# A convolution module in which ScalarE and VectorE follow the written order and SyncE issues every copy

## Chip, cores and metric

The kernel runs on one core of a Trainium2 chip. The metric is device time in microseconds (us) of one execution; the profile's span is the stretch from the first to the last instruction of one profiled execution.

## What is computed

A two-layer decoder trunk on 256 tokens of width 1024, in float32. Each layer has a half-step SwiGLU feed-forward network (FFN, inner width 2816), a token mixer, and a second FFN. The mixer of layer 0 is the Conformer convolution module, which the change is about; that of layer 1 is stick-breaking attention. The module computes, with h the normalized input:

```python
val, gate = split(h @ w_pw1 + b_pw1, 2)
u = val * sigmoid(gate)
u = depthwise_causal_conv(u, w_dw, width=31) + b_dw
u = silu(layer_norm(u, ln_g, ln_b))
x = x + u @ w_pw2 + b_pw2
```

## The kernel before

Tokens lie in T = 2 tiles of 128. All large products are made in pieces: each float32 weight is loaded as `raw` and split into a rounded part `hi` (a cast on ScalarE, line 144) and the rest `lo` (a subtraction on VectorE, line 145), and `mm3` (lines 180 to 182) adds three matmuls, hi x hi, lo x hi, hi x lo, into one PSUM tile. `raw` has three buffers, `hi` and `lo` six each, for the whole kernel. SyncE (SP in the profile) issues the loads of the weights.

The module (`conv`) has 1024 channels, in eight blocks k of 128 (up, acc, sk). Its steps are:

- **U(e, t)**, for four chunks e of w_pw1 and two token tiles t: 24 matmuls with the chunk's two halves (four k each), then ScalarE copies the sum to `vg`, scaled (line 401). Each U leaves a **gate** behind: four transposes of vg on PE (line 406), and for the chunk's two channel blocks a sigmoid `sg` on ScalarE (line 409) and a multiply-add `up` on VectorE (line 410). The gate of one U is put into the middle of the next U (after nine matmuls) or of the next taps.
- **shifted(k, ...)**: four copies, SBUF to SBUF, by DMA of `up[k]` to `sk[k]`, which lays four shifted copies of 32 channels over the partitions (line 441). Odd k are issued by ScalarE, even k by SP.
- **weights(e)**: two VectorE products `wb` (line 426), the banded weights of the convolution.
- **taps(k, tb, nt)**: the depthwise convolution of a block as matmuls of sk[k] with wb (line 451), 64 rows in the trace, then `acc` is copied from PSUM by ScalarE with the bias (line 457). The first four blocks are done for both token tiles at once, the last four once for each tile. The narrow ones take turns on two PSUM buffers with U.
- **norm_in, norm, turn, out_mm**: transposes of acc and `bn_stats` (line 470), the layer norm as two VectorE steps `z` and a sigmoid times z (`m`, lines 484 to 489), transposes of m and a split to `xT` (line 496), the second product (lines 180 to 182) and its addition to x (line 509).
- **boundary**: the normalized, transposed input of the next FFN.

The program order at the end of `conv` decides what is issued when: inside `tc.manual_schedule` the engines named in its list take their instructions as written. Before, that list is PE and SP. ScalarE, VectorE and GpSimd are ordered by the framework's scheduler when the kernel is built. Each engine then runs its own list strictly in order. A tile whose buffer is not yet free makes the instruction that writes it wait.

Of the kernel before, what the change touches and what calls it, by code (L numbers as in the profile page):

```python
# [8 lines left out]
F32 = mybir.dt.float32  # L9
F32R = mybir.dt.float32r  # L10
# [4 lines left out]
P = 128  # L15
D = 1024
KD = D // P
T = 2
DFF = 2816
# [13 lines left out]
def trunk_kernel(  # L33
# [7 lines left out]
    nc = tc.nc  # L41
# [97 lines left out]
    def nm(s):  # L139
        uid[0] += 1  # L140
        return f"{s}_{uid[0]}"

    def split(hi, lo, src, eng=None, copy=nc.scalar.copy):
        copy(hi, src)  # L144
        (eng or nc.vector).tensor_tensor(lo, src, hi.bitcast(F32), op=ALU.subtract)  # L145
# [20 lines left out]
    def load_pairs(w, c0, c1, n, **kw):  # L166

        wv = w.rearrange("(k p) n -> p k n", p=P)
        return [
            load_w([wv[:, 4 * h : 4 * h + 4, c : c + n] for c in (c0, c1)], [4, 2, n], **kw) for h in range(2)  # L170
        ]

    def load_rows(w, k0, **kw):

        wv = w.rearrange("(k p) n -> p k n", p=P)
        hi, lo = load_w([wv[:, k0 : k0 + 2, :]], [2, 1, D], **kw)
        return hi[:, :, 0, :], lo[:, :, 0, :]
# [33 lines left out]
    def u_mm(t, hT, units, n, between=None):  # L211
        ps = ps_u.tile([P, 512], F32, tag="u", name=nm("psu"))
        h, l, _ = hT
        for k in range(KD):
            wh, wl = units[k // 4]
            mm3(ps[:, :n], h[:, k, :], l[:, k, :], wh[:, k % 4], wl[:, k % 4], k == 0, k == KD - 1)
            if between is not None and k == 2:
                between()
        return ps
# [153 lines left out]
        return outs  # L373


    def conv(hTs, next_gi):
        H = TAPS
        SW = H - 3 + T * P
        acc = [
# [2 lines left out]
        up, sks, wbs, vunits = [], {}, [], []  # L382
        units = {}

        def load_chunk(e):
            units[e] = load_pairs(conv_w_pw1[0], 2 * e * P, D + 2 * e * P, 2 * P, pieces=4)

        def load_out(c):
            vunits.append(load_rows(conv_w_pw2[0], 2 * c))

        pending = []

# [2 lines left out]
            if pending:  # L395
                pending.pop()()

        def U(e, t):
            ps = u_mm(t, hTs[t], units[e], 512, between=finish)
            vg = wk.tile([P, 4, P], F32, tag="B", bufs=4, name=nm("vg"))  # L400
            nc.scalar.activation(vg, ps, AF.Copy, scale=hTs[t][2])

            def gate():
                pt = ps_t.tile([P, 4, P], F32, tag="tr", name=nm("ptr"))
                for q in range(4):
                    nc.tensor.transpose(pt[:, q, :], vg[:, q, :], ident)
                for q, k in enumerate((2 * e, 2 * e + 1)):
                    s = wk.tile([P, P], F32, tag="sg", name=nm("sg"))
                    nc.scalar.activation(s, pt[:, 2 + q, :], AF.Sigmoid, bias=vec[:, B1 + 8 + k : B1 + 9 + k])
                    nc.vector.scalar_tensor_tensor(  # L410
                        up[k][:, H + t * P : H + (t + 1) * P],
                        pt[:, q, :], vec[:, B1 + k : B1 + k + 1], s, op0=ALU.add, op1=ALU.mult,
                    )
                    if e == 3:
                        shifted(k, *((0, SW - P), (SW - P, SW))[t])
                    elif t == T - 1:
                        shifted(k, 0, SW)

            pending.append(gate)

        def weights(e):

            wb = ring.tile([P, 2, 32, 32], F32, tag=("hi", "lo")[e % 2], name=nm("wb"))
            for i in range(2):
                k = 2 * e + i
                nc.vector.tensor_tensor(
                    wb[:, i],
                    ind.unsqueeze(1).broadcast_to([P, 32, 32]),
                    wq[:, 4 * k : 4 * k + 4, :].rearrange("p g m -> p (g m)").unsqueeze(2)
                    .broadcast_to([P, 32, 32]),  # L430
                    op=ALU.mult,
                )
            wbs.append(wb)

        def shifted(k, a, b):

            if k not in sks:
                sks[k] = wk.tile([P, 4, SW], F32, tag="sk", bufs=4, name=nm("sk"))
            for g in range(4):
                v = up[k][32 * g : 32 * g + 32, a:b]  # L440
                (nc.scalar if k % 2 else nc.sync).dma_start(
                    sks[k][:, g, a:b], bass.AP(tensor=v.tensor, offset=v.offset, ap=[v.ap[0], [1, 4], [1, b - a]])
                )

        def taps(k, tb, nt, pool, tag):
            wb, sk = wbs[k // 2][:, k % 2], sks[k]
            pc = pool.tile([P, nt * P], F32, tag=tag, name=nm("pc"))
            for m in range(8):
                for g in range(4):
                    c = 4 * m + tb * P  # L450
                    nc.tensor.matmul(  # L451
                        pc[32 * g : 32 * g + 32, :], wb[:, 8 * g + m, :], sk[:, g, c : c + nt * P],
                        start=m == 0, stop=m == 7,
                    )
                if m == 3:
                    finish()
            nc.scalar.activation(
                acc[k][:, tb * P : (tb + nt) * P], pc, AF.Identity, bias=vec[:, BD + k : BD + k + 1]
            )
# [3 lines left out]
        def norm_in(t, q):  # L463

            if t not in stats:
                stats[t] = wk.tile([P, 2, 6], F32, tag="st", name=nm("st"))
            pl = ps_v.tile([P, 4, P], F32, tag=f"v{t}{q}", name=nm("pl"))
            for i in range(4):
                nc.tensor.transpose(pl[:, i, :], acc[4 * q + i][:, t * P : (t + 1) * P], ident)
            nc.vector.bn_stats(stats[t][:, q, :], pl.rearrange("p k c -> p (k c)"))  # L470
            pls[t, q] = pl
# [28 lines left out]
        def out_mm(t, n):  # L500
            ns = slice(n * 512, (n + 1) * 512)
            pv = ps_v.tile([P, 512], F32, tag=f"v{t}{n}", name=nm("psv"))
            for k in range(KD):
                wh, wl = vunits[k // 2]
                mm3(
                    pv, xT[:, t, k, 0, :], xT[:, t, k, 1, :], wh[:, k % 2, ns], wl[:, k % 2, ns],
                    k == 0, k == KD - 1,
                )
            nc.vector.tensor_tensor(xt[t][:, ns], pv, xt[t][:, ns], op=ALU.add)

        for _ in range(KD):
            up.append(wk.tile([P, H + T * P], F32, tag="A", bufs=13, name=nm("up")))
            nc.gpsimd.memset(up[-1][:, :H], 0.0)
        outs = []


        with tc.manual_schedule(engines={mybir.EngineType.PE, mybir.EngineType.SP}):
            load_chunk(0)
            load_chunk(1)
            U(0, 0)  # L520
            weights(0)
            U(0, 1)
            load_chunk(2)
            U(1, 0)
            weights(1)
            load_chunk(3)
            U(1, 1)
            b2 = wk.tile([P, D], F32, tag="sc4", name="b2")
            nc.sync.dma_start(b2, conv_b_pw2[0:1, :].broadcast_to([P, D]))
            taps(0, 0, T, ps_v, "v01")  # L530
            U(2, 0)
            load_out(0)
            taps(1, 0, T, ps_v, "v11")
            weights(2)
            U(2, 1)
            for t in range(T):
                nc.vector.tensor_tensor(xt[t], xt[t], b2, op=ALU.add)
            taps(2, 0, T, ps_v, "v01")
            U(3, 0)
            weights(3)  # L540
            for c in range(1, 4):
                load_out(c)
            taps(3, 0, T, ps_v, "v11")
            U(3, 1)
            taps(4, 0, 1, ps_v, "v01")
            norm_in(0, 0)
            taps(5, 0, 1, ps_v, "v11")
            taps(6, 0, 1, ps_u, "u")
            taps(7, 0, 1, ps_u, "u")
            taps(4, 1, 1, ps_u, "u")  # L550
            norm_in(0, 1)
            norm(0)
            taps(5, 1, 1, ps_u, "u")
            norm_in(1, 0)
            taps(6, 1, 1, ps_u, "u")
            turn(0, 0)
            taps(7, 1, 1, ps_u, "u")
            turn(0, 1)
            norm_in(1, 1)
            norm(1)  # L560
            out_mm(0, 0)
            out_mm(0, 1)
            for q in range(2):
                turn(1, q)
            out_mm(1, 0)
            outs.append(boundary(0, next_gi))
            out_mm(1, 1)
        outs.append(boundary(1, next_gi))
        return outs


    def attention(hTs, next_gi):
# [155 lines left out]
    ]  # L728
    hTs.append(boundary(1, 0))
    hTs = ffn(0, 0, 0, hTs, 1, first=first, hook=load_conv_consts)  # L730
    hTs = conv(hTs, 2)
    hTs = ffn(0, 1, 2, hTs, 3)
    hTs = ffn(1, 0, 3, hTs, 4)
    hTs = attention(hTs, 5)
    nc.sync.dma_start(fg, final_g.rearrange("(o d) -> o d", o=1).broadcast_to([P, D]))
# [27 lines left out]
```

## Time and profile before

| | |
|---|---|
| Time, median of 3 runs | 1014.5 us (1012.63 to 1016.3) |
| Profiled execution, own time | 1018.19 us |
| Its span | 1016.3 us |
| PE busy | 984.6 us |
| VectorE (DVE) busy | 710.4 us |
| ScalarE (ACT) busy | 515.3 us |
| mean granted clock of TensorE | 0.992 |
| convolution module on PE | about 202 us to 329 us of the span |

Reading it: a row of the timeline has the start in us, the duration, the engine, the line, the operation and `out<-in`, then how often it is repeated; in brackets stands how long the engine was idle before it and which instruction ended the wait. ACTq and SPq are the sequencers of ScalarE and SP issuing DMAs; while ScalarE issues, it does nothing else. Matmuls overlap, so the start-to-start distance is what one costs.

### The profile page before, as it was taken

How to read it: one execution, taken by the hardware profiler on the slowest of the kernel's cores; microseconds unless marked ns; L12 is line 12 of the kernel's file. 1: busy time of each engine (PE TensorE's matmuls, PEld its weight loads, DVE VectorE, ACT ScalarE, POOL GpSimd, SP SyncE). 2: the span in 40 equal slices, each digit the busy share in tenths (PEclk: the TensorE clock that was granted, in tenths of full speed). 3: DMA queues.
4: the chain of work that ended last, by engine and by line, in shares of the span. 5: the costliest groups of instructions: out<-in, count | busy, mean ns of one | idle time of the engine just before them, and what ended most of it. 6: DMA issues, size and time to landing. Idle time of an engine off the chain costs nothing.

```text
span 1016.3 us, 14823 instructions
## 1 busy us (share of the span) xinstructions
PE 984.6 (97%) x5710; PEld 816.8 (80%) x5710; DVE 710.4 (70%) x1094; ACT 515.3 (51%) x870; POOL 142.6 (14%) x173
## 2 busy tenths in 40 slices
PE   6999999998889999999999999999999999999997
PEld 5888888875578888888888888888777678888885
DVE  6977777845346877776787777777767986767664
ACT  5654545433333645454555454555644554545432
POOL 5011111100000111111111111111210011111111
PEclk9999999998989999999999999999999999999999
DMA  8857564434652764747465647474625346555511
GB/s 272 295 181 251 171 230 148 158 97 141 193 192 68 244 227 148 234 145 238 148 188 165 227 148 235 145 235 145 190 87 180 108 129 203 180 193 190 183 42 42
DMA packets 143111, 177.76 MB, mean 175 GB/s; under 512 B 6392, under 2 KB 126272, under 8 KB 143040
## 3 DMA queue, kind: packets, MB, share of 16 engines
q1 hardware_dynamic: 139808, 173.93, 52.8%
q10 hardware_dynamic: 3232, 2.88, 1.1%
q8 instruction: 45, 0.74, 0.3%
q14 instruction: 26, 0.21, 0.1%
HBM read 171.08 MB, written 1.05 MB: 169 GB/s over the span
## 4 chain that ended last, share of the span: by engine, by line
PE 87%; DMA 4%; DVE 3%; ACT 2%; issue 1%; SPq 1%; ACTq 1%; POOL 0%; POOLq 0%; DVEq 0%
PE psc L228 28%; PE psc L229 16%; PE psv L180 8%; PE psv L182 8%; PE psv L181 8%; PE psc L231 4%; PE psu L180 3%; PE psu L181 2%; PE psu L182 2%; PE pc L451 2%; DMA raw<-in_conv_w_pw_dram 2%; DMA raw<-in_ffn_w_in_dram 2%; DVE lo L145 1%; ACT hi L144 1%; PE pz L620 1%
## 5 line engine op out<-in xcount | busy, mean ns | idle before, releaser
L145 DVE TENSOR_TENSOR lo<-raw,hi 128x1024 fp32r<-128x1024 f32 (+1 forms) x352 | 398.2, 1150 | 117.5 <-ACT hi L144 117.0
L228 PE MATMUL psc<-xT,hi 128*128 128x512 f32 x1232 | 443.0, 398 | 0.6 <-DVE u L234 0.6
L144 ACT CAST hi<-raw 128x1024 fp32r<-128x1024 f32 (+1 forms) x356 | 327.6, 960 | 106.8 <-PE psc L228 35.2
L229 PE MATMUL psc<-xT,lo 128*128 128x256 f32 x1408 | 366.7, 281 | 0.0
L229 PEld LDWEIGHTS psc<-xT,lo 128*128 128x128 f32 x1408 | 265.6, 189 | 16.0 <-issue 0.4
L228 PEld LDWEIGHTS psc<-xT,hi 128*128 128x128 f32 x1232 | 231.8, 188 | 50.8 <-DVE u L234 1.0
L289 POOL TENSOR_TENSOR s<-s,rrow 128x256 f32<-128x256 f32 x80 | 93.9, 1173 | 585.1 <-DVE s L288 585.1
L180 PE MATMUL psv<-hi,ah 128*128 128x512 f32 x352 | 137.6, 391 | 0.1
L181 PE MATMUL psv<-lo,ah 128*128 128x512 f32 x352 | 137.2, 390 | 0.0
L182 PE MATMUL psv<-hi,al 128*128 128x512 f32 x352 | 136.9, 390 | 0.0
L233 ACT COPY u<-psc 128x256 f32<-128x256 f32 x176 | 65.2, 371 | 132.1 <-PE psc L231 131.7
L234 DVE TENSOR_TENSOR u<-psc,u 128x256 f32<-128x256 f32 x176 | 74.0, 421 | 79.3 <-ACT u L233 78.7
L144 ACT CAST ah<-s 128x256 fp32r<-128x256 f32 x80 | 32.6, 407 | 95.8 <-DVE s L291 95.8
L181 PEld LDWEIGHTS psv<-lo,ah 128*128 128x128 f32 x352 | 66.1, 188 | 14.0
L182 PEld LDWEIGHTS psv<-hi,al 128*128 128x128 f32 x352 | 66.1, 188 | 13.9
L180 PEld LDWEIGHTS psv<-hi,ah 128*128 128x128 f32 x352 | 66.1, 188 | 12.9 <-ACT ah L144 1.0
L231 PE MATMUL psc<-xT,hi 128*128 128x512 f32 x176 | 70.0, 398 | 0.0
L180 PE MATMUL psu<-hi,xT 128*128 128x512 f32 x160 | 65.0, 406 | 0.0
L181 PE MATMUL psu<-lo,xT 128*128 128x512 f32 x160 | 63.3, 396 | 0.0
L182 PE MATMUL psu<-hi,xT 128*128 128x512 f32 x160 | 63.0, 394 | 0.0
L287 ACT ACTIVATE s<-u 128x256 f32<-128x256 f32 x80 | 33.3, 416 | 46.5 <-DVE u L285 46.5
L145 DVE TENSOR_TENSOR al<-s,ah 128x256 fp32r<-128x256 f32 x80 | 33.5, 419 | 21.8 <-ACT ah L144 21.8
(128 smaller groups left out, 791.2 us busy)
## 6 DMA issues: line engine op xcount, KB each, us to landing
raw<-in_ffn_w_in_dram SPq DMA_DIRECT2D x172, 512.0 KB, 4.7
raw<-in_ffn_w_out_dram SPq DMA_DIRECT2D x44, 1024.0 KB, 4.9
raw<-in_conv_w_pw_dram SPq DMA_DIRECT2D x16, 512.0 KB, 4.5
raw<-in_attn_w_qkv_dram SPq DMA_DIRECT2D x16, 512.0 KB, 4.6
raw<-in_conv_w_pw_dram SPq DMA_DIRECT2D x4, 1024.0 KB, 7.9
raw<-in_attn_w_qkv_dram SPq DMA_DIRECT2D x4, 1024.0 KB, 5.1
raw<-in_attn_w_o_dram SPq DMA_DIRECT2D x4, 1024.0 KB, 4.9
raw<-in_ffn_w_in_dram SPq DMA_DIRECT2D x8, 256.0 KB, 5.8
```

What stands on the lines that cost most here:

```text
L144: copy(hi, src)
L145: (eng or nc.vector).tensor_tensor(lo, src, hi.bitcast(F32), op=ALU.subtract)
L180: nc.tensor.matmul(ps, lh, rh, start=start, stop=False)
L181: nc.tensor.matmul(ps, lh, rl, start=False, stop=False)
L182: nc.tensor.matmul(ps, ll, rh, start=False, stop=stop)
L228: nc.tensor.matmul(ps, h, xT[:, :, k, :, :], start=k == 0, stop=False)
L229: nc.tensor.matmul(ps[:, :, 0, :], l, xT[:, :, k, 0, :], start=False, stop=False)
L231: nc.tensor.matmul(ps, h, xT[:, :, k, :, :], start=False, stop=True)
L233: nc.scalar.copy(u, ps[:, :, 1, :])
L234: nc.vector.tensor_tensor(u, ps[:, :, 0, :], u, op=ALU.add)
L287: nc.scalar.activation(a, u, AF.Sigmoid)
L289: nc.gpsimd.tensor_tensor(a, a, rrow, op=ALU.mult)
```

## The change

All of it is in `conv` and its two callers:

- the list of engines in `manual_schedule` now names ScalarE and VectorE too;
- loading and casting a weight unit are two functions, `fetch_*` and `cast`, called at different places: the fetch of a half chunk stands some steps ahead, its cast inside the U of the chunk before it, behind that U's gate and any `weights` (through the new arguments of U);
- all copies of `shifted` are issued by SP;
- the fetches and casts of the next FFN's first unit (both halves) stand inside `conv`, and the FFN is handed the result;
- the addition of b_pw2 to x stands behind taps(5, 0).

```diff
-    def conv(hTs, next_gi):
+    def conv(hTs, next_gi, next_w):
...
+        def fetch(srcs, shape):
+            raw = rawp.tile([P, *shape], F32, tag="raw", name=nm("raw"))
+            for c, src in enumerate(srcs):
+                nc.sync.dma_start(raw[:, :, c, :], src)
+            return [raw, shape]
+
+        def cast(unit):
+            raw, shape = unit
+            hi = ring.tile([P, *shape], F32R, tag="hi", name=nm("hi"))
+            lo = ring.tile([P, *shape], F32R, tag="lo", name=nm("lo"))
+            for k in range(shape[0]):
+                split(hi[:, k], lo[:, k], raw[:, k])
+            unit[:] = hi, lo
...
-        def U(e, t):
-            ps = u_mm(t, hTs[t], units[e], 512, between=finish)
+        def U(e, t, *todo):
+            def between():
+                finish()
+                for f, *args in todo:
+                    f(*args)
+
+            ps = u_mm(t, hTs[t], units[e], 512, between=between)
...
-                (nc.scalar if k % 2 else nc.sync).dma_start(
+                nc.sync.dma_start(
...
-        with tc.manual_schedule(engines={mybir.EngineType.PE, mybir.EngineType.SP}):
-            load_chunk(0)
-            load_chunk(1)
-            U(0, 0)
-            weights(0)
-            U(0, 1)
-            load_chunk(2)
-            U(1, 0)
-            weights(1)
-            load_chunk(3)
-            U(1, 1)
...
+        E = mybir.EngineType
+        with tc.manual_schedule(engines={E.PE, E.SP, E.Activation, E.DVE}):
+            fetch_in(0, 0)
+            fetch_in(0, 1)
+            fetch_in(1, 0)
+            for unit in units[0]:
+                cast(unit)
+            fetch_in(1, 1)
+            fetch_in(2, 0)
+            U(0, 0, (cast, units[1][0]))
+            fetch_in(2, 1)
+            U(0, 1, (cast, units[1][1]))
+            fetch_in(3, 0)
+            U(1, 0, (weights, 0), (cast, units[2][0]))
+            fetch_in(3, 1)
             b2 = wk.tile([P, D], F32, tag="sc4", name="b2")
             nc.sync.dma_start(b2, conv_b_pw2[0:1, :].broadcast_to([P, D]))
+            U(1, 1, (cast, units[2][1]))
+            fetch_out(0)
             taps(0, 0, T, ps_v, "v01")
-            U(2, 0)
-            load_out(0)
+            U(2, 0, (weights, 1), (cast, units[3][0]))
+            fetch_out(1)
             taps(1, 0, T, ps_v, "v11")
-            weights(2)
-            U(2, 1)
+            U(2, 1, (cast, units[3][1]))
+            fetch_out(2)
+            taps(2, 0, T, ps_v, "v01")
+            U(3, 0, (weights, 2), (cast, vunits[0]), (cast, vunits[1]))
+            fetch_out(3)
+            nxt.append(fetch_chunk(next_w, 0, DFF, 0))
+            taps(3, 0, T, ps_v, "v11")
+            U(3, 1, (weights, 3), (cast, vunits[2]))
+            nxt.append(fetch_chunk(next_w, 0, DFF, 1))
+            taps(4, 0, 1, ps_v, "v01")
+            norm_in(0, 0)
+            cast(vunits[3])
+            taps(5, 0, 1, ps_v, "v11")
             for t in range(T):
                 nc.vector.tensor_tensor(xt[t], xt[t], b2, op=ALU.add)
...
             taps(7, 0, 1, ps_u, "u")
+            cast(nxt[0])
             taps(4, 1, 1, ps_u, "u")
...
             out_mm(0, 0)
+            cast(nxt[1])
             out_mm(0, 1)
...
-    hTs = ffn(0, 1, 2, hTs, 3)
+    hTs, first = conv(hTs, 2, ffn_w_in[0, 1])
+    hTs = ffn(0, 1, 2, hTs, 3, first=first)
```

How the order moves, at three places. The numbers behind the names tell buffers apart and are not the same in both programs.

ScalarE around the U of chunk 1 and token tile 1 and the first taps, before (vg_2127 and vg_2194 are the copies of U(1,0) and U(1,1), hi_2133 and hi_2146 the two halves of chunk 3, acc_1909 the result of the first taps):

```order
L441 DMA sk_2107<-up_1919 128x1x284 x4
L401 ACTIVATE vg_2127<-psu_2081,rstd_285_1862 128x512
L409 ACTIVATE sg_2173<-ptr_2168,vec 128x128
L409 ACTIVATE sg_2176<-ptr_2168,vec 128x128
L144 CAST hi_2133<-raw_2132 128x512 x4
L401 ACTIVATE vg_2194<-psu_2158,rstd_293_1907 128x512
L144 CAST hi_2146<-raw_2145 128x512 x4
L409 ACTIVATE sg_2220<-ptr_2215,vec 128x128
L457 ACTIVATE acc_1909<-pc_2198,vec 128x256
```

and now (vg_2120 and vg_2173 are the copies of U(1,0) and U(1,1), hi_2095 and hi_2148 the halves of chunk 2, hi_2245 the first half of chunk 3):

```order
L144 CAST hi_2095<-raw_1967 128x512 x4
L425 ACTIVATE vg_2120<-psu_2061,rstd_285_1862 128x512
L433 ACTIVATE sg_2142<-ptr_2137,vec 128x128
L433 ACTIVATE sg_2145<-ptr_2137,vec 128x128
L144 CAST hi_2148<-raw_2007 128x512 x4
L425 ACTIVATE vg_2173<-psu_2127,rstd_293_1907 128x512
L433 ACTIVATE sg_2199<-ptr_2194,vec 128x128
L433 ACTIVATE sg_2207<-ptr_2194,vec 128x128
L481 ACTIVATE acc_1909<-pc_2177,vec 128x256
L144 CAST hi_2245<-raw_2058 128x512 x4
```

The four copies are gone from ScalarE's list, and the cast ahead of the vg of U(1,1) is now that of chunk 2; the cast of chunk 3 stands behind the first taps.

ScalarE around the layer norm of token tile 0, before (acc_1913 to acc_1916 are blocks 4 to 7, here from the narrow taps; m_2765 and m_2771 the sigmoids of norm(0); hi_3110 the second half of the next FFN's first unit; xT the split of turn):

```order
L457 ACTIVATE acc_1916<-pc_2684,vec 128x128
L457 ACTIVATE acc_1913<-pc_2718,vec 128x128
L457 ACTIVATE acc_1914<-pc_2776,vec 128x128
L488 ACTIVATE m_2765<-z_2764 128x512
L144 CAST hi_3110<-raw_3109 128x512 x3
L488 ACTIVATE m_2771<-z_2770 128x512
L457 ACTIVATE acc_1915<-pc_2817,vec 128x128
L144 CAST hi_3110<-raw_3109 128x512
L144 CAST xT<-ptr_2851 128x4x128
L457 ACTIVATE acc_1916<-pc_2858,vec 128x128
```

and now (hi_2724 is the first half of the next FFN's first unit):

```order
L481 ACTIVATE acc_1916<-pc_2690,vec 128x128
L144 CAST hi_2724<-raw_2457 128x512 x4
L481 ACTIVATE acc_1913<-pc_2734,vec 128x128
L512 ACTIVATE m_2781<-z_2780 128x512
L512 ACTIVATE m_2787<-z_2786 128x512
L481 ACTIVATE acc_1914<-pc_2792,vec 128x128
L481 ACTIVATE acc_1915<-pc_2833,vec 128x128
L144 CAST xT<-ptr_2867 128x4x128
L481 ACTIVATE acc_1916<-pc_2874,vec 128x128
```

acc_1914, the result of taps(5,1), stood ahead of both sigmoids and now stands behind both; four casts now stand between the last acc of tile 0 and the first of tile 1.

SP around the copies of the last pair of blocks, before (sk_2499 is block 6; raw_2450 to raw_2466 are pieces of w_pw2, raw_3096 and raw_3109 the next FFN's first unit):

```order
L159 DMA raw_2450<-in_conv_w_pw_dram 128x2x1024
L159 DMA raw_2458<-in_conv_w_pw_dram 128x2x1024
L159 DMA raw_2466<-in_conv_w_pw_dram 128x2x1024
L441 DMA sk_2499<-up_1929 128x1x156 x4
L159 DMA raw_3096<-in_ffn_w_in_dram 128x4x256 x2
L159 DMA raw_3109<-in_ffn_w_in_dram 128x4x256 x2
L159 DMA raw_3122<-in_ffn_w_out_dram 128x2x1024
L441 DMA sk_2499<-up_1929 128x1x128 x4
```

and now (sk_2485 and sk_2493 are blocks 6 and 7, raw_2455 the last piece of w_pw2, raw_2457 and raw_2551 the next FFN's first unit):

```order
L388 DMA raw_2455<-in_conv_w_pw_dram 128x2x1024
L388 DMA raw_2457<-in_ffn_w_in_dram 128x4x256 x2
L465 DMA sk_2485<-up_1929 128x1x156 x4
L465 DMA sk_2493<-up_1931 128x1x156 x4
L388 DMA raw_2551<-in_ffn_w_in_dram 128x4x256 x2
L465 DMA sk_2485<-up_1929 128x1x128 x4
L465 DMA sk_2493<-up_1931 128x1x128 x4
```

Both blocks' copies now stand in this one list, sixteen with two loads between them, and the first FFN loads stand ahead of them.

## Rows read from the trace of the kernel before

**Rows 1.** The page, its first part: busy time, share, instructions.

```profile
PE 984.6 (97%) x5710; PEld 816.8 (80%) x5710; DVE 710.4 (70%) x1094; ACT 515.3 (51%) x870; POOL 142.6 (14%) x173
```

**Rows 2.** Waits with PE waiting, 196 to 345 us: total, times, longest.

```profile
PE ptr L406 <- ACT vg L401: 10.2, 3, 5.0
PE pc L451 <- ACT acc L457: 3.0, 1, 3.0
```

**Rows 3.** Timeline of PE: first and second pause.

```profile
223.31 0.66 PE L406 MATMUL ptr<-ident,vg 128*128 128x128 f32 x4 [0.91 <-ACT vg L401]
...
233.52 1.12 PE L406 MATMUL ptr<-ident,vg 128*128 128x128 f32 x4 [4.24 <-ACT vg L401]
...
239.22 0.39 PE L180 MATMUL psu<-hi,xT 128*128 128x512 f32 x1
```

**Rows 4.** Timeline of PE: the same place at full clock, to the next taps.

```profile
255.96 0.66 PE L406 MATMUL ptr<-ident,vg 128*128 128x128 f32 x4
...
259.23 0.40 PE L180 MATMUL psu<-hi,xT 128*128 128x512 f32 x1
...
264.12 1.93 PE L451 MATMUL pc<-sk,wb 128*32 128x256 f32 x32
```

**Rows 5.** Timeline of PE: third and fourth pause, and full clock between.

```profile
280.27 1.11 PE L406 MATMUL ptr<-ident,vg 128*128 128x128 f32 x4 [5.05 <-ACT vg L401]
...
283.18 0.66 PE L469 MATMUL pl<-ident,acc 128*128 128x128 f32 x4
283.76 5.45 PE L451 MATMUL pc<-sk,wb 128*32 128x128 f32 x192
292.16 2.55 PE L451 MATMUL pc<-sk,wb 128*32 128x128 f32 x64 [2.95 <-ACT acc L457]
...
298.08 0.66 PE L469 MATMUL pl<-ident,acc 128*128 128x128 f32 x4
```

**Rows 6.** Busy time by stretch; the first number after POOL is the granted clock.

```profile
234.00:236.00 2.00, 2.00 (x19) 0.98 (x22) 1.98 (x4) 1.82 (x4) 0.00 (x0) 0.50 0.01 2
254.00:256.00 2.00, 2.00 (x34) 0.98 (x33) 0.72 (x1) 0.69 (x1) 0.00 (x0) 1.00 0.00 0
294.00:296.00 2.00, 2.00 (x28) 1.27 (x23) 0.21 (x1) 0.37 (x1) 0.56 (x3) 0.50 0.98 333
```

**Rows 7.** Timeline of ScalarE: copies issued, a cast, acc, a sigmoid of the norm.

```profile
218.58 3.95 ACTq L441 DMA_DIRECT2D sk<-up  x4
...
230.71 2.18 ACT L144 CAST hi<-raw 128x512 fp32r<-128x512 f32 x4 [5.49 <-DMA raw<-in_conv_w_pw_dram]
...
287.61 3.83 ACTq L441 DMA_DIRECT2D sk<-up  x4
291.49 0.88 ACT L457 ACTIVATE acc<-pc,vec 128x128 f32<-128x128 f32 x3 [4.62 <-issue]
...
300.59 0.63 ACT L488 ACTIVATE m<-z 128x512 f32<-128x512 f32 x1
```

**Rows 8.** SP's timeline; the tile sk; issues by line with KB and landing.

```profile
257.54 4.29 SPq L441 DMA_DIRECT2D sk<-up  x4
...
L441 SPq DMA_DIRECT2D sk<-up x20: 542/602/2024, 217.8 to 289.3; - x20
...
DMA to landing us min/median/max: 2.2/4.0/6.5
...
raw<-in_conv_w_pw_dram SPq DMA_DIRECT2D x4, 1024.0 KB, 7.9
```

**Rows 9.** Timeline of VectorE: lo behind the cast of rows 7; norm(0).

```profile
231.36 2.50 DVE L145 TENSOR_TENSOR lo<-raw,hi 128x512 fp32r<-128x512 f32 x4 [5.75 <-ACT hi L144]
...
295.79 0.70 DVE L470 BATCH_NORM_STATS2 st<-pl 128x6 f32<-128x512 f32 x1 [7.62 <-PE pl L469]
...
299.14 0.69 DVE L489 TENSOR_TENSOR m<-z,m 128x512 f32<-128x512 f32 x1
299.75 0.75 DVE L487 SCALAR_TENSOR_TENSOR z<-z,lnr,lnb 128x512 f32<-128x512 f32 x1
```

More of the change, by code (lines that the diff above doesn't have):

```diff
@@ L383, in conv, with fetch_chunk, fetch_in, fetch_out @@
         units = {}
[L385 to L389, printed above, removed]
+        def fetch(srcs, shape):
[10 more added lines that the diff above has]
+            unit[:] = hi, lo
+        def fetch_chunk(w, c0, c1, h):
+            wv = w.rearrange("(k p) n -> p k n", p=P)
+            return fetch([wv[:, 4 * h : 4 * h + 4, c : c + 2 * P] for c in (c0, c1)], [4, 2, 2 * P])
+        def fetch_in(e, h):
+            units.setdefault(e, []).append(fetch_chunk(conv_w_pw1[0], 2 * e * P, D + 2 * e * P, h))
+        def fetch_out(c):
+            wv = conv_w_pw2[0].rearrange("(k p) n -> p k n", p=P)
+            vunits.append(fetch([wv[:, 2 * c : 2 * c + 2, :]], [2, 1, D]))
         pending = []
@@ L505, in out_mm @@
                 mm3(
-                    pv, xT[:, t, k, 0, :], xT[:, t, k, 1, :], wh[:, k % 2, ns], wl[:, k % 2, ns],
+                    pv, xT[:, t, k, 0, :], xT[:, t, k, 1, :], wh[:, k % 2, 0, ns], wl[:, k % 2, 0, ns],
                     k == 0, k == KD - 1,
@@ L513, in conv @@
             nc.gpsimd.memset(up[-1][:, :H], 0.0)
-        outs = []
-        with tc.manual_schedule(engines={mybir.EngineType.PE, mybir.EngineType.SP}):
-            load_chunk(0)
-            load_chunk(1)
-            U(0, 0)
-            weights(0)
-            U(0, 1)
-            load_chunk(2)
-            U(1, 0)
-            weights(1)
-            load_chunk(3)
-            U(1, 1)
+        outs, nxt = [], []
+        E = mybir.EngineType
[13 more added lines that the diff above has]
+            fetch_in(3, 1)
@@ L536, in conv @@
             for t in range(T):
                 nc.vector.tensor_tensor(xt[t], xt[t], b2, op=ALU.add)
[L538 to L547, printed above, removed]
             taps(6, 0, 1, ps_u, "u")
             taps(7, 0, 1, ps_u, "u")
+            cast(nxt[0])
@@ L568, in conv @@
         outs.append(boundary(1, next_gi))
-        return outs
+        return outs, nxt
     def attention(hTs, next_gi):
@@ L730, in trunk_kernel @@
     hTs = ffn(0, 0, 0, hTs, 1, first=first, hook=load_conv_consts)
-    hTs = conv(hTs, 2)
-    hTs = ffn(0, 1, 2, hTs, 3)
+    hTs, first = conv(hTs, 2, ffn_w_in[0, 1])
+    hTs = ffn(0, 1, 2, hTs, 3, first=first)
     hTs = ffn(1, 0, 3, hTs, 4)
```

## The prediction

> **What bounds the kernel now.** The page's first part comes first: PE is busy for 97% of the span [rows 1], so only a PE that stands still, or runs slowly, can give time back. The second view is the list of waits with PE as the one that waits, over the convolution module (196 to 345 us): PE stood still there for 10.2 us in front of the gate's transposes, three times, always for ScalarE's copy vg, and once for 3.0 us in front of taps, for ScalarE's acc [rows 2]. The third is PE's timeline, where the four pauses have their places: 0.91 us in U(1,1), 4.24 us in the first taps [rows 3], 5.05 us in the first taps of the half width and 2.95 us ahead of taps(4,1) [rows 5]. That is 13.15 us.
>
> A pause costs more than itself. After 4.24 us of standing still the granted clock is 0.50, the lower of the two levels (1.2 GHz), against 1.00 before; the same after the 2.95 us [rows 6]. From the gate's transposes to the fourth matmul of the next U takes 5.70 us there (233.52 to 239.22) [rows 3], and 3.27 us in the same place at full clock (255.96 to 259.23) [rows 4]: 2.43 us lost. After the 5.05 us, the transposes and 32 tap rows take 2.91 us (280.27 to 283.18); at full clock four transposes take 0.58 and 32 rows 5.45/6 = 0.91 [rows 5], together 1.49: 1.42 us lost. After the 2.95 us, 64 tap rows, four transposes and 64 tap rows take 5.92 us (292.16 to 298.08) instead of 2 x 1.82 + 0.58 = 4.22 [rows 5]: 1.70 us lost. After 0.91 us nothing is lost. Together 5.55 us.
>
> The fourth view is ScalarE's timeline, for the reason behind "ACT vg" and "ACT acc" [rows 7]. ScalarE takes its instructions in order. It spends 3.95 us issuing four copies while vg waits behind them (the 0.91), it stands 5.49 us in front of a cast whose weights have not landed, with vg behind the cast (the 4.24), and it spends 3.83 us issuing copies while three acc wait (the 2.95). The 5.05 is the same again: copies that wait for VectorE's up, with a cast between them, ahead of vg.
>
> **The change, part by part.** *Copies off ScalarE's queue.* The 20 copies that ScalarE issues go to SP, which now issues 40. This removes the reason of the 0.91, of the 5.05 and of the 2.95 us. What it adds on SP: four copies take up to 4.29 us of its queue [rows 8], so the second channel block of a pair starts some 4 us later than before. What hides this is the distance to the taps that read it: the last pair is the tightest. SP can begin it 1.6 us after the gate's transposes (255.96 to 257.54) [rows 4, 8]. From those transposes to the end of the next U are 8.16 us [rows 4], then taps(4,0) to taps(7,0) are 0.91 + 0.58 + 0.91 + 0.58 + 5.45 = 8.43 us [rows 5]. Taps(7,0), the last 1.82 of these, needs eight copies by 13.2 us after SP began; at 0.60 us an issue (the median) and 4.0 us to landing [rows 8] they are there after 8.8, at 4.29 for four after 12.6. I cost it at nothing; the bound on the other side is below, as a rival.
>
> The Trainium skill ("DMA: Bandwidth & Descriptors", section "Issuing engines are not separate DMA queues") says that copies started by different engines share the same 16 DMA engines, and that using several engines saves only the time of starting them, usually small beside the transfer. By its first half nothing is lost by the move; its second half speaks against the move here, since 4.29 us for four starts is not small beside a 4.0 us landing [rows 8]. The sum is zero by the rule and by the median row.
>
> *Loads ahead of copies, casts a chunk ahead.* Chunk 3's first half was issued behind the first copies and landed at 230.7, when ScalarE already stood at its cast [rows 7]. Now its issue stands ahead of these copies on SP, and its cast stands in U(2,0), after vg(1,1). Between lie the rest of U(1,0), U(1,1) and taps(0): 15 matmuls, 24 with a gate, and taps with a gate. At 0.233 us a matmul (21 take 4.89, 259.23 to 264.12), 0.58 for a gate and 2.0 for half of the taps (8.16 less 0.58 and 24 matmuls) [rows 4, 5] that is 3.5 + 6.2 + 4.6 = 14.3 us, against 7.9 us that even the 1 MB loads take to land [rows 8]. That removes the 4.24 us. A later load's issue waits only for a cast that is now a chunk early, so I cost the fetches of w_pw2 and of the next FFN's first unit at nothing: their cover is one whole U with taps, 5.6 + 4.6 = 10.2 us.
>
> *ScalarE and VectorE in written order.* Up to taps(4,0) the order costs nothing by my walk: four casts take 2.18 us [rows 7], behind a gate stand 15 matmuls of its U, 3.5 us, and vg is not wanted before nine matmuls of the next U are done, 2.1 us more; the gate's two sigmoids and ups (1.6 us from the gate's start to SP's) [rows 4, 8] and the casts are 3.8 us of these 5.6. After it, it costs. Count from E, the end of taps(7,0). ScalarE does acc(7,0), about 0.4 (three take 0.88) [rows 7], then the four casts of the next FFN's first half; VectorE has their lo 3.15 us after the first cast starts (230.71 to 233.86) [rows 7, 9]. So bn_stats starts at E + 3.55, though its input is there at E + 2.4. From bn_stats to the end of m(0,0) are 4.04 us (295.79 to 299.83) [rows 9]: E + 7.6. PE reaches turn(0,0) at E + 3 x 1.82 + 2 x 0.58 = E + 6.6: a **wait of 1.0 us**. ScalarE's order then has both sigmoids ahead of acc(5,1), which frees the PSUM buffer of taps(7,1). The second needs two more z steps of 0.75 and takes 0.63 [rows 7, 9]: E + 7.6 + 2.13, and 0.3 for acc is E + 10.0. PE is through with turn(0,0) at E + 8.2: a **wait of 1.8 us**. Before, the scheduler let acc(5,1) pass the sigmoids, and no wait stands there. In all 2.8 us of new waits.
>
> No row shows what the clock does after 1.0 and 1.8 us with 0.6 us of work between. The nearest rows are nothing after 0.91 us, 1.70 after 2.95 us [rows 3, 5]. Together they are 2.8 us, so I take 1.7 and keep 0 for the range. The later chain to norm(1) has out_mm(0,0) and out_mm(0,1), 48 matmuls, over it, and costs nothing.
>
> **Sum.** Gained 13.15 + 5.55 = 18.7; given back 2.8 + 1.7 = 4.5; net 14.2 us. The profiled execution took 1018.19 us with a span of 1016.3, so it would take 1004.0 with a span of 1002.1. It is 3.7 us above the median of the runs shown; off the median of 1014.5 the forecast is **1000.3 us**.
>
> **The rivals.**
> 1. *The new waits don't come, or the clock stays up.* For: they rest on chains put together from rows in another order. Against: the order of ScalarE is plain. 1014.5 - 18.7 = 995.8 without waits, 998.6 with waits but without the slow spell.
> 2. *One early pause stays*: a cast on ScalarE stands again in front of weights that land late, vg behind it, now since ScalarE's order is fixed. For: the cast that waited shows DMA as its releaser [rows 7]. Against: the 14.3 us of lead. Price: 4.24 + 2.43 = 6.7, so 1007.0.
> 3. *Both pauses in front of vg stay*, so that the change does not do what it says: 5.05 + 1.42 = 6.5 more, 1013.5, no change.
> 4. *SP becomes the limit, slower than before.* Place: the last pair. Between SP's start and the forecast start of taps(7,1) lie 8.16 - 1.6 + 8.43 + 10.0 = 25.0 us, in which SP makes 16 copies and two loads. At 0.60 us each and 4.0 to landing that is 14.8. At the slowest issue and the slowest landing of any copy, 2.02 and 6.5 us [rows 8], it is 42.9: 17.9 us late, and a second slow spell of 2.4: 1020.6. It makes the kernel slower from about 1.7 us an issue on (18 x 1.7 + 6.5 is 12.1 late, with 2.4 the whole net gain). For: each SP copy now waits for an earlier transfer of its queue slot, loads among them. Against: the median and the longest group of four, 1.07 us each.
>
> The skill's rule on issuing engines lowers rival 4's chance as far as the transfers go, and raises it as far as the starts go; I leave it low.
>
> **How the numbers follow.** Forecast 0.49, rival 1 0.20, rival 2 0.16, rival 3 0.07, rival 4 0.08. About 0.3%, 3.0 us, is what a measurement of this kernel can tell from no change. Faster: 0.49 + 0.20 + 0.16 = 0.85; same: 0.07; slower: 0.08. The range takes in rival 1 at the low end and rival 2 at the high end, with 1 to 2 us for the spread of the runs (1012.63 to 1016.3): 994 to 1008. Left out are rivals 3 and 4, 0.15.
>
> **What would show it.** Right: no wait of PE for vg over 0.5 us; the granted clock at 1.00 from 202 us to taps(7,0); out_mm(0,0) starting about 14 us earlier than the 304.1 of before; two new waits, of turn(0,0) on VectorE's m and of taps(7,1) on ScalarE's acc, with lower clock behind them. Wrong: PE waits for sk (rival 4), casts with a DMA as releaser ahead of vg (rivals 2, 3), or an FFN behind the module that starts with a wait, which the sum holds at none since its first unit is cast earlier than U needs it and the buffers of the rest come free with out_mm(1,1) as before.

## The result, and the profile after

The changed kernel takes **1003.35 us** (median of 4 runs, 1001.39 to 1005.28), beside 1015.4 us (4 runs, 1012.63 to 1017.07) for the kernel before in the same rounds: a ratio of 0.9884 with an interval of 0.9852 to 0.9916. It is faster by 12.05 us. The forecast was 14.2 us faster, and the range of 994 to 1008 holds the time.

The profiled execution took 1002.38 us. Its page answers to [rows 1] with these lines: busy time by engine, then the chain that ended last.

```profile
span 1000.6 us, 14813 instructions
PE 979.1 (98%) x5710; PEld 813.8 (81%) x5710; DVE 711.9 (71%) x1094; ACT 514.9 (51%) x870; POOL 142.3 (14%) x173
...
PE 92%; DVE 2%; ACT 2%; DMA 2%; issue 1%; SPq 0%; POOL 0%; POOLq 0%; ACTq 0%; DVEq 0%
```

PE now makes up 92% of the chain (87% before) and DMA 2% (4% before). The list of PE's waits over the module answers to [rows 2]:

```profile
PE pc L475 <- ACT acc L481: 1.8, 1, 1.8
PE ptr L520 <- DVE m L513: 0.8, 1, 0.8
PE psv L180 <- ACT xT L144: 0.2, 1, 0.2
```

No wait for vg is left. The two others are the two that the prediction named. PE's timeline has their places; the windows behind it have the granted clock in the third column from the end.

```profile
269.95 7.19 PE L475 MATMUL pc<-sk,wb 128*32 128x128 f32 x256
...
282.87 0.66 PE L520 MATMUL ptr<-ident,m 128*128 128x128 f32 x4 [0.78 <-DVE m L513]
285.29 1.95 PE L475 MATMUL pc<-sk,wb 128*32 128x128 f32 x64 [1.77 <-ACT acc L481]
```

```profile
282.00:284.00 2.00, 0.75 (x8) 0.42 (x4) 1.84 (x3) 0.09 (x1) 0.42 (x1) 1.00 0.78 266
284.00:286.00 2.00, 0.71 (x28) 0.71 (x32) 1.25 (x3) 1.62 (x4) 0.00 (x0) 1.00 0.03 9
286.00:288.00 2.00, 2.00 (x56) 1.80 (x44) 0.91 (x2) 0.50 (x2) 0.00 (x0) 1.00 0.03 8
```

The first row is 256 tap rows without a pause, where the kernel before has the 5.05 and the 2.95 us [rows 5]. The clock stayed at 1.00 through the two waits that are left. SP's timeline, beside the 4.29 us for four copies of [rows 8], shows eight in 5.3 to 6.6 us:

```profile
218.29 5.25 SPq L465 DMA_DIRECT2D sk<-up  x8
...
260.17 6.57 SPq L465 DMA_DIRECT2D sk<-up  x8
```

For the reading below I measure **the module**: on PE, from the first transposes of the boundary ahead of it (line 204) to the first of the boundary behind it. That is 196.79 to 321.99 = 125.20 us before and 197.22 to 306.15 = 108.93 us after, 16.27 less. The rows at the two ends, of before and then of after:

```profile
196.79 0.60 PE L204 MATMUL ptr<-ident,x 128*128 128x128 f32 x4
...
321.99 1.03 PE L204 MATMUL ptr<-ident,x 128*128 128x128 f32 x8
```

```profile
197.22 0.60 PE L204 MATMUL ptr<-ident,x 128*128 128x128 f32 x4
...
306.15 1.03 PE L204 MATMUL ptr<-ident,x 128*128 128x128 f32 x8
```

The two profiled spans differ by 15.7 us, the medians by 12.05; where the other 4 us are is one of the questions for the experiments.

### The profile page after: what moved, and what is told of

It is laid out like the page before. It is cut to its first block, busy times and chain, and to the rows that moved or that the text cites. A ratio compares the mean times of both kernels' runs of the same rounds, so it can differ in the third digit from the quotient of the medians.

```text
span 1000.6 us, 14813 instructions
## 1 busy us (share of the span) xinstructions
PE 979.1 (98%) x5710; PEld 813.8 (81%) x5710; DVE 711.9 (71%) x1094; ACT 514.9 (51%) x870; POOL 142.3 (14%) x173
## 4 chain that ended last, share of the span: by engine, by line
PE 92%; DVE 2%; ACT 2%; DMA 2%; issue 1%; SPq 0%; POOL 0%; POOLq 0%; ACTq 0%; DVEq 0%
PE psc L228 28%; PE psc L229 16%; PE psv L180 8%; PE psv L182 8%; PE psv L181 8%; PE psc L231 4%; PE psu L180 4%; PE psu L181 4%; PE psu L182 4%; PE pc L475 2%; DMA raw<-in_ffn_w_in_dram 1%; PE ptr L204 1%; PE pz L653 1%; ACT hi L144 1%; PE pwo L180 1%
```

## The experiments

Times with several runs are medians, with the interval of the ratio to the kernel before, taken in the same rounds on the same chip. e1, e2, e3, e4, e8, e10 and e11 ran once, and a single time can stand 2 us off its own median. Each edit is to the changed kernel unless it says otherwise.

| run | module, us | PE's waits in the module over 0.25 us | time, us |
|---|---|---|---|
| before | 125.20 | vg 10.2, acc 3.0 | 1015.4 |
| e10, before again | 120.75 | vg 8.0, acc 2.5 | 1015.06 |
| after | 108.93 | acc 1.8, m 0.8 | 1003.35 |
| e5, after again | 109.87 | issue 2.0, acc 0.7 | 1003.45 (0.9873 to 0.9907) |
| e1, odd copies on ScalarE | 119.56 | vg 5.4, acc 1.9, issue 1.0, m 1.0 | 1013.99 |
| e2, only the copies moved | 115.51 | vg 4.4, issue 1.6 | 1008.34 |
| e12, chunk 3 fetched late | 109.62 | acc 1.8, m 0.5, issue 0.3 | 1003.24 (0.9871 to 0.9925) |
| e3, scheduler's order | 107.34 | issue 0.7 | 1000.43 |
| e7, the same again | 110.61 | issue 2.7 | 1002.22 (0.9862 to 0.9898) |
| e4, norm and casts later | 108.12 | xT 1.6 | 1001.9 |
| **e6, the same, casts later still** | **106.55** | none | **1001.02 (0.9848 to 0.9881)** |
| e9, e6 with two loads more | 107.59 | issue 0.9 | 1001.37 (0.9857 to 0.989) |
| e8, one more ScalarE copy | 109.87 | acc 2.7 | 1003.74 |
| e11, two more | 113.46 | acc 3.7, m 0.8 | 1006.43 |

**Which part of the change gains.** Theory: the pauses went because ScalarE no longer issues copies *and* no longer stands at casts whose weights are late. Rivals: the copies alone did it, or the written order of ScalarE and VectorE did. e1 puts the odd copies back on ScalarE:

```diff
-                nc.sync.dma_start(
+                (nc.scalar if k % 2 else nc.sync).dma_start(
```

> The changed kernel with one line back: the copies of the odd blocks are issued by ScalarE again. Measure: the module's length on PE, from the first transposes of its input (boundary, 197.2 us in the changed kernel) to the first transposes of the next boundary (306.2): 108.9 us changed, 125.2 before. Theory A (ScalarE's issuing of copies made the pauses): four copies of 2.6 to 3.9 us ahead of the casts push vg(1,0) some 2.7 us past the moment at which the gate wants it, and acc(6,0) past taps(4,1) by as much; module 115 to 117 us, the clock at 0.50 behind at least one of the pauses. Theory B (late loads and the place of the casts made them): no wait of PE for vg over 0.5 us, module under 111 us.

e2 takes the kernel before and moves the copies alone (the same line the other way):

> The kernel before with one line changed: all copies of shifted are issued by SP; the engines' order stays the scheduler's, loads and casts stay together. Theory A (copies on ScalarE made the pauses): module 109 to 112 us, nearly the whole gain. Theory B (loads that stand behind copies on SP, with casts in front of vg): the loads of chunk 3 now stand behind eight copies, and those of three pieces of w_pw2 too; the wait ahead of vg(3,1) stays at 4 us or more with its slow spell, module 113 to 118 us. Theory C (written order is what counts): module over 118 us.

With the odd copies back on ScalarE 10.6 us of module return (119.56 against 108.93), more than the 115 to 117 us of theory A, and the waits for vg with them. ScalarE's timeline in e1 has the four copies and a cast ahead of vg, and PE's the longest wait behind them:

```profile
219.26 3.95 ACTq L465 DMA_DIRECT2D sk<-up  x4
223.25 2.18 ACT L144 CAST hi<-raw 128x512 fp32r<-128x512 f32 x4 [4.41 <-issue]
```

```profile
226.07 1.12 PE L430 MATMUL ptr<-ident,vg 128*128 128x128 f32 x4 [3.00 <-ACT vg L425]
```

Of the 10.6 us, 5.4 are waits for vg and some 1.5 the slow clock behind this one. Another 1.0 are pauses named "issue" and some 1.2 a slow spell behind a wait of 1.77 us for acc that the changed kernel has too; those need not come from the copies. The acc of block 6, which theory A saw late as well, cost 0.16 us.

With the copies alone 115.51 us are reached, and one long wait for vg stays, in the place of the 5.05 us of before. ScalarE's timeline in e2 shows its reason:

```profile
263.98 2.00 ACT L144 CAST hi<-raw 128x1024 fp32r<-128x1024 f32 x2 [7.13 <-DMA raw<-in_conv_w_pw_dram]
...
268.96 1.99 ACT L144 CAST hi<-raw 128x1024 fp32r<-128x1024 f32 x2 [0.20 <-DMA raw<-in_conv_w_pw_dram]
270.86 0.68 ACT L401 ACTIVATE vg<-psu,rstd 128x512 f32<-128x512 f32 x1
```

```profile
271.59 1.11 PE L406 MATMUL ptr<-ident,vg 128*128 128x128 f32 x4 [4.43 <-ACT vg L401]
```

Six casts of w_pw2 stand ahead of vg, and the weights of the first two landed late; 4.43 us of PE behind them, as in the second reason of [rows 7]. The other three pauses are gone in e2, the 4.24 us too, though chunk 3 is loaded late as before. The scheduler, which orders ScalarE anew for each program, has put vg ahead of the waiting cast there:

```profile
226.10 0.69 ACT L401 ACTIVATE vg<-psu,rstd 128x512 f32<-128x512 f32 x1 [2.24 <-PE psu L182]
229.98 2.19 ACT L144 CAST hi<-raw 128x512 fp32r<-128x512 f32 x4 [3.19 <-DMA raw<-in_conv_w_pw_dram]
```

So both parts are needed, and neither's gain is a number of its own: whichever reason stays, a vg stands behind it.

**The early fetch, or the place of the cast.** e12 issues the fetch of chunk 3's first half behind the copies again and leaves its cast where the change put it:

```diff
-            fetch_in(3, 0)
             U(1, 0, (weights, 0), (cast, units[2][0]))
+            fetch_in(3, 0)
             fetch_in(3, 1)
```

> The changed kernel, but the fetch of chunk 3's first half stands behind U(1,0) again, so that SP issues it behind the copies of the gate before, as in the kernel before: about 224 us instead of 215.7. Its cast stays where the change put it, at about 231.5. Theory A (the early fetch is what removed the pause of 4.24 us): ScalarE stands 1 to 3 us in front of the cast with DMA as its releaser, and PE waits for vg again at about 237 to 240 us, 1 us or more; time 1 to 5 us above the changed kernel's 1003.4. Theory B (putting the cast behind vg(1,1), a whole U ahead of its use, is what removed it): ScalarE has 3.1 us to spare ahead of vg(2,0), so even a cast that starts 2 us late keeps PE from waiting; no wait of PE for vg over 0.3 us, time within 1 us of 1003.4.

Theory B held: no wait for vg, and 1003.24 us. SP issued the four loads from 223.48 on, and ScalarE's cast starts where it did, without a wait:

```profile
223.48 3.72 SPq L388 DMA_DIRECT2D raw<-in_conv_w_pw_dram  x4
```

```profile
231.41 2.17 ACT L144 CAST hi<-raw 128x512 fp32r<-128x512 f32 x4
236.72 0.69 ACT L425 ACTIVATE vg<-psu,rstd 128x512 f32<-128x512 f32 x1 [3.13 <-PE psu L182]
```

For this chunk the cast's place behind vg(1,1), a U ahead of its use, is enough, as it was in e2; of the 14.3 us of lead that the prediction reckoned, 8 can go. Whether the early fetch would have been enough with the cast in its old place was not run.

**The written order of ScalarE and VectorE.** e3, and e7 with more runs, give both back to the scheduler:

```diff
-        with tc.manual_schedule(engines={E.PE, E.SP, E.Activation, E.DVE}):
+        with tc.manual_schedule(engines={E.PE, E.SP}):
```

> The changed kernel with the list of engines in written order as before (PE and SP alone): the scheduler orders ScalarE and VectorE, fetches, casts and copies stay as changed. If written order is a part of the gain (theory C): pauses of PE for vg or acc come back, module 112 us or more. If it only costs (my theory): the two new waits of 0.78 and 1.77 us go, none comes, module 106.3 to 107.5 us, and the gain comes from the copies and from the fetches ahead.

> e3_sched again, timed: the changed kernel with ScalarE and VectorE in the scheduler's order. Module 107.3 us in its first trace, so about 1.6 us less than the changed kernel on the same chip; if written order is worth something in other executions, it is slower than the changed kernel.

The waits for m and acc are gone in both. e3's module is as expected, and its single time is 1000.43 us; e7's is 3.3 us longer than the 107.3 expected, by the pause of 2.67 us treated below and the slow clock behind it. e7's median is 1002.22 us, 1.2 below the changed kernel's 1003.45 (e5) in the same rounds; the two spreads, 1002.15 to 1003.77 and 1003.18 to 1004.21, overlap in one run. The written order is not where the gain comes from; it costs about 1 us. e4 and e6 keep it and change what is written: norm(0) behind taps(5,1), so that acc(5,1) passes its sigmoids, and the casts of the next FFN's first unit later.

```diff
             taps(7, 0, 1, ps_u, "u")
-            cast(nxt[0])
             taps(4, 1, 1, ps_u, "u")
             norm_in(0, 1)
-            norm(0)
             taps(5, 1, 1, ps_u, "u")
+            norm(0)
...
             out_mm(0, 0)
-            cast(nxt[1])
+            cast(nxt[0])
             out_mm(0, 1)
             for q in range(2):
                 turn(1, q)
+            cast(nxt[1])
```

That is e6; e4 has both casts behind out_mm(0,0) instead.

> The changed kernel with two calls moved: norm(0) stands behind taps(5,1) instead of ahead of it, so that acc(5,1) stands ahead of both sigmoids on ScalarE, and the cast of the next FFN's first half stands behind out_mm(0,0) with that of the second. By the forecast's chain both new waits go (0.78 and 1.77): module 106.4 us, with nothing lost in the next FFN. If the waits come from the length of the chain from bn_stats to m instead, the wait of turn(0,0) stays at 0.5 us or more and the module is above 107.5 us.

> The changed kernel with norm(0) behind taps(5,1), the cast of the next FFN's first half behind out_mm(0,0), and that of the second half behind turn(1,0) and turn(1,1). In e4_norm_cast VectorE did both halves' eight lo ahead of turn's lo and PE waited 1.55 us for it; four of them move behind it here. Expected: no wait over 0.3 us in the module, 106.4 to 106.8 us, the FFN behind it without a new wait, and about 2.4 us less than the changed kernel on the same chip. If VectorE is full there, the wait moves into the next FFN's first U.

In e4 both waits are gone, but PE stands 1.55 us inside a later product, for VectorE's part of xT, since eight lo in a row are ahead of it:

```profile
299.80 0.50 PE L182 MATMUL psv<-hi,xT 128*128 128x512 f32 x1 [1.55 <-DVE xT L145]
```

e6 mends that too. At 1001.02 us (1000.69 to 1001.24) it **beats both kernels**, 2.4 us below the changed kernel in the same rounds (e5, lowest run 1003.18), and its module of 106.55 us is the shortest seen.

**The spread: does the module always take as long?** e5 is the changed kernel again, e10 the kernel before.

> The changed kernel itself, for the second time. Its trace showed the module 16.3 us shorter, and its four runs a median 12.05 us lower. If the module's length is the gain and the rest is spread between executions, the gain here is 13 to 17 us and the trace again shows 0.78 and 1.77 us of waits with the module at 108.9 to 110.7 us. If the clock behind the two waits falls in some executions (it fell behind 1.03 and 1.77 us in e1_odd_on_act, and not in the changed kernel's trace), the runs lie up to 1.7 us apart from it more than those of the kernel before, and this trace may show it.

> The kernel before, unchanged. From its first boundary transposes ahead of the module to the first behind it the profiled execution took 125.2 us, the changed kernel's 108.9, 109.9 in a second execution. If the profiled execution of before was a long one of its own (the medians differ by 12.0 us, the two profiled spans by 15.7), the module here takes 121 to 124 us, with its pauses in front of vg and acc 1 to 4 us shorter than 13.15 together, or with fewer rows at half clock. If the gain that the medians lack is lost outside the module, it takes 125 again.

e5's gain, 1015.41 - 1003.45 = 11.96 us, lies below the 13 to 17 expected, and of the two waits only 0.67 us for acc came, with 2.0 us of pauses named "issue" ahead of it. The module of before took 120.75 us in e10, just under the 121 to 124 of the first expectation and 4.45 less than in the profile that the prediction read. The same waits are there, all but the first shorter. PE's timeline, and the granted clock around the second and the last of them (230 to 232 has the pause itself):

```profile
224.18 0.66 PE L406 MATMUL ptr<-ident,vg 128*128 128x128 f32 x4 [1.16 <-ACT vg L401]
232.69 0.66 PE L406 MATMUL ptr<-ident,vg 128*128 128x128 f32 x4 [2.53 <-ACT vg L401]
...
277.90 1.11 PE L406 MATMUL ptr<-ident,vg 128*128 128x128 f32 x4 [4.30 <-ACT vg L401]
289.51 1.96 PE L451 MATMUL pc<-sk,wb 128*32 128x128 f32 x64 [2.48 <-ACT acc L457]
```

```profile
230.00:232.00 2.00, 0.15 (x4) 0.00 (x0) 1.48 (x3) 2.00 (x5) 0.00 (x0) 1.00 1.08 401
234.00:236.00 2.00, 2.00 (x24) 1.08 (x20) 2.00 (x5) 1.13 (x3) 0.00 (x0) 0.50 0.00 0
...
290.00:292.00 2.00, 2.00 (x64) 1.64 (x52) 0.00 (x0) 0.37 (x1) 0.42 (x1) 1.00 0.84 240
```

The pauses add up to 1.16 + 2.53 + 4.30 + 2.48 = 10.47 us instead of 13.15, and after the last one the clock stays at 1.00. The module less pauses is 120.75 - 10.47 = 110.28, which is 3.73 us above e6's 106.55: that is left, mostly for the slow clock, instead of 5.55. By the prediction's own terms the first execution gives 125.20 - 18.7 = 106.5, the same base. So a changed kernel with 109 to 110 us is 11 to 16 us ahead, depending on the execution of before that it is held against; the medians say 12.05.

**The pause called "issue".** In e5 PE stood still for 2.0 us, in e7 for 2.7 us, in the middle of dense tap rows, with no releaser that the profile names. PE's timeline of e5:

```profile
272.95 5.22 PE L475 MATMUL pc<-sk,wb 128*32 128x128 f32 x174 [0.59 <-issue]
...
283.11 1.73 PE L475 MATMUL pc<-sk,wb 128*32 128x128 f32 x55 [1.44 <-issue]
```

Theory: PE's instructions come late. The DMA queue called instruction moved 45 packets, 0.74 MB, in the span; PE has 2 x 5710 matmuls and weight loads, 254 for each packet, so the queue q8 is taken to be PE's. Half-width taps use a packet up in 3.6 us (127 rows of 7.19/256). In e7 the q8 packets of this stretch lie in the windows of 1 us from 267, 275, 279 and 284 us, with one gap of 8; in that gap the DMA engines are full (share 1.03 from 271 to 274), and PE stands still until 278.06. First the line of the DMA view of 275 to 276 us (packets, MB, share of 16 engines), then PE's timeline:

```profile
q8 instruction: 1, 0.02, 5.9%
```

```profile
269.76 5.63 PE L475 MATMUL pc<-sk,wb 128*32 128x128 f32 x199
278.06 2.07 PE L475 MATMUL pc<-sk,wb 128*32 128x128 f32 x49 [2.67 <-issue]
```

e9 makes the DMA engines full on purpose in e6, which has a q8 packet every 4 us there and no such pause:

```diff
+            for i in range(2):
+                ex = wk.tile([P, KD, P], F32, tag="sc4", name=nm("ex"))
+                nc.sync.dma_start(ex, next_w.rearrange("(k p) n -> p k n", p=P)[:, :, i * P : (i + 1) * P])
```

> The kernel of e6 with two loads of 512 KB more on SP, in pieces of 512 bytes, into scratch tiles that nobody reads, put behind the last copies, so that they and the 1 MB load of w_out behind them fill the stretch of the half-width taps of token tile 1. In it PE fetches a block of instructions about every 4 us (packets of the queue q8 instruction). Theory A (those packets wait behind the data when the DMA share is near 1, and PE runs out of instructions): PE stands still with issue as its releaser for 1.5 to 5 us in that stretch, where e6 had none, a q8 packet there is 2 to 4 us later than its neighbours' distance of 4, and the time is 1.5 to 5 us above e6's 1001.0. Theory B (the pauses put down to issue come from elsewhere, such as the ScalarE and VectorE order): no such pause, 1001.0 within 0.7.

The packet due at 280 us came at 283, and 2.9 us behind the start of that window PE came out of a pause of 0.91 us. PE's timeline, and the DMA view of 283 to 284 us:

```profile
284.37 0.66 PE L520 MATMUL ptr<-ident,m 128*128 128x128 f32 x4 [0.20 <-DVE m L513]
285.94 0.60 PE L493 MATMUL pl<-ident,acc 128*128 128x128 f32 x4 [0.91 <-issue]
```

```profile
q8 instruction: 1, 0.02, 7.4%
```

The direction is theory A's, the size is below its 1.5 to 5 us: 0.91 us in the trace, and 1001.37 against 1001.02 us cannot be told apart. That a packet came late while the DMA engines were full, and that a pause followed, is shown in one execution of e9. The traces bear out the tie between packet and pause: the module has 12 pauses named "issue" in all the runs, and each ends 2.3 to 2.7 us behind a q8 packet (placed by DMA views of 0.1 us), in e5 behind those at 270.5 and 280.6. That full DMA engines are what delayed each of these packets is likely, not shown.

**What a pause does to the clock.** e8 puts one ScalarE copy of 128x1024 ahead of acc(5,1), e11 two:

```diff
+            for _ in range(1):
+                nc.scalar.copy(wk.tile([P, D], F32, tag="sc4", name=nm("spin")), xt[1])
             taps(5, 1, 1, ps_u, "u")
```

> The changed kernel with one more ScalarE instruction, a copy of 128x1024 into a tile that nothing reads, ahead of acc(5,1): it makes the wait of taps(7,1) some 1.05 us longer, 2.8 us with the 0.78 ahead of it. If such a wait drops the clock as the 2.95 us did in the kernel before, the granted clock falls to 0.50 behind it and the module grows by 1.05 + 1.7 us to 111.7; if the clock stays, by 1.05 to 110.0.

> The changed kernel with two copies of 128x1024 on ScalarE ahead of acc(5,1); one copy made the wait of taps(7,1) 2.67 us long instead of 1.77 and left the granted clock at 1.00. Now the wait is some 3.5 us. If the clock falls by the length of the pause alone, with its bound between 2.67 (clock stayed) and 2.95 (clock fell, kernel before), it falls here: 0.50 to 0.75 in a window behind the wait, and 64 tap rows take about 2.5 to 3.2 us instead of 1.8; the module is 2 to 3 us longer than with one copy. If what counts is more than the pause, the clock stays at 1.00 and the module is 0.9 us longer.

The rows of PE's timeline behind the wait, of e8 and then of e11, and two windows of e11 with the granted clock:

```profile
286.15 1.95 PE L475 MATMUL pc<-sk,wb 128*32 128x128 f32 x64 [2.67 <-ACT acc L481]
```

```profile
286.29 3.64 PE L475 MATMUL pc<-sk,wb 128*32 128x128 f32 x64 [3.66 <-ACT acc L481]
```

```profile
286.00:288.00 2.00, 1.71 (x33) 1.58 (x36) 0.69 (x1) 0.97 (x3) 0.00 (x0) 0.50 0.00 0
288.00:290.00 2.00, 2.00 (x39) 1.52 (x30) 0.00 (x0) 0.00 (x0) 0.00 (x0) 0.50 0.03 8
```

After 2.67 us 64 rows take 1.95, after 3.66 us 3.64. e8's module is as expected for a clock that stays; e11's is 3.6 us longer, above the 2 to 3 expected: 1.0 us of longer wait, 0.8 of a wait for m that e8 does not have, and some 2 of slow rows. But the length of the pause alone does not decide: e10 has the clock at 0.50 after 2.53 us and at 1.00 after 2.48, and e7 falls to 0.50 behind the 2.67 us for which e8 stays at 1.00. A window of e7:

```profile
280.00:282.00 2.00, 2.00 (x25) 1.55 (x28) 0.76 (x2) 0.37 (x1) 0.56 (x3) 0.50 0.88 255
```

What else decides is open.

## Why the prediction was right, and where its sizes were off

- **Pauses in front of vg and acc (13.15 us).** Right: none of the four is left. Their reason, ScalarE's queue with copies and with casts of late weights in it, is shown by e1 and e2. Which reason belongs to which pause was not right throughout: the prediction let the copies' move take away the 5.05 us and the early loads and casts the 4.24, but with the copies alone moved (e2) the 4.24 went and 4.43 of the 5.05 stayed, behind casts of w_pw2.
- **Slow clock behind them (5.55 us).** Right for the profile it was read from: 18.7 us taken from that module leave 106.5, which is what e6 measures with no waits (106.55). Too large as a term of the median, with the pauses: e10 has 10.47 and 3.73, together 14.2 instead of 18.7. **This is the step that failed in size.** The sum took 18.7 us from an execution that lay 3.7 us above the median of the runs, and then subtracted them from the median; but the two executions of before that have a profile differ by just such pauses. In the comparison of the medians some 14 us were there to gain; e6, which has no wait left, lies 14.4 us below the kernel before in its rounds.
- **The two new waits (2.8 us).** Right in place, cause and size in the trace of after: 0.78 + 1.77 = 2.55. Other executions have less, e12 0.5 and 1.8, e5 only 0.67. Counted from the end of taps(7,0), bn_stats was forecast 3.55 us behind and m's end 7.6; with that end at 275.4 (192 of the 256 rows from 269.95) they come 3.4 and 7.4 us behind in VectorE's timeline:

```profile
278.79 0.69 DVE L494 BATCH_NORM_STATS2 st<-pl 128x6 f32<-128x512 f32 x1
...
282.12 0.69 DVE L513 TENSOR_TENSOR m<-z,m 128x512 f32<-128x512 f32 x1 [0.70 <-ACT m L512]
```

- **A slow spell of 1.7 us behind them.** Did not come in the trace of after; the clock stayed at 1.00. It can come: e1 has waits of 1.03 and 1.77 us in the same place, and its next 64 rows take 3.17 us. Rival 1's second case, waits without the slow spell, is what the profile shows: 18.7 - 2.8 = 15.9 forecast, 16.27 measured, between the modules of the two profiled executions.
- **The copies on SP at nothing.** Right. Forty copies took SP 0.60 us each at the median, and no tap waited for sk. Rival 4 falls with it. The Trainium skill ("DMA: Bandwidth & Descriptors", section "Issuing engines are not separate DMA queues") calls the time of starting a transfer usually small beside it. On ScalarE here it was not: four starts took 3.95 us [rows 7] beside 4.0 us to landing [rows 8], and with the odd copies back in its queue PE waited 5.4 us for vg (e1). The measurement decides; the rule says nothing of what stands behind a start.
- **Loads ahead of copies.** Right that the pause goes, half right in why: by e12 and e2 the cast's place behind vg is enough, and the early fetch was not needed for it.
- **Rivals 2 and 3** (a pause for vg stays) did not come in any execution of the changed kernel seen.
- **What the sum had no term for**: 0 to 2 us of "issue" pauses, different from execution to execution.

Of the gain, 12.05 us came where 14.2 were forecast. By e10's numbers 18.7 - 14.2 = 4.5 us too much were held to be gained, and 1.95 too much to be given back (1.7 of slow clock, 0.25 of waits): 14.2 - 4.5 + 1.95 = 11.65. That the two errors have opposite signs and nearly half cancel is luck. The 0.4 us left over are less than the runs' spread; the pauses of the last point would take from the gain, and how much they take from the median is open. The median of before was 0.9 us higher in these rounds than in those that the forecast started from, so the time itself lies 3.05 us above it.

## What to carry to other kernels

An engine that copies results out of PSUM should not issue DMAs or meet a cast whose weights may be late: put the DMA copies on a queue whose other work can wait for them, and each cast behind the last urgent copy out of PSUM, one step ahead of its use. When an engine is taken from the scheduler, walk its list for short work that frees a PSUM buffer and stands behind a chain that waits for another engine; the moves of e6, norm(0) and two casts together, were worth 2.4 us here. Take the sizes of pauses from more than one execution, or scale them to the median before subtracting them from it.

## What the runs showed that was not expected

- PE can run out of instructions, as far as the pauses named "issue" show. With the DMA engines full, a packet of the instruction queue came 3 to 4 us late in e7 and e9, and PE paused 2.7 and 0.9 us among narrow matmuls that use up a packet in 3.6 us. The Trainium skill ("Runtime: NRT & Kernel Launch", section "Instruction fetch mechanics") says that the sequencer fetches blocks of 16 KiB ahead by its own DMA queue and that crossing to the next one is mostly hidden. The size agrees (0.74 MB in 45 packets); in these stretches the crossing was not hidden.
- The kernel before varies by its pauses: its module took 125.20 and 120.75 us in two executions with the same instructions.
- Pauses of nearly the same length left the clock alone (2.48, 2.67 us) or brought it down to 0.50 behind them (2.53, 2.67 us).
